# Attention of 16 heads: from half-head steps under a planner to 128 written slots

## Chip, core and metric

The kernel runs on one core of one Trainium2 chip. The metric is the device time of one execution in microseconds (us). Shapes are fixed: 1024 tokens, width 1024, 16 heads of 64, a feed-forward width of 2816, everything in float32.

## What is computed

One block of a network: a causal convolution branch and an attention branch, both fed by one normalised input, are gated and added, and a feed-forward part follows. Cut to the part that matters here:

```python
h = rms_norm(x, norm1_g)
z = h @ w_in                                  # glu_in | q | k | v | gate_logits
a = a_val * sigmoid(a_gate)
a = silu(rms_norm(causal_depthwise_conv(a, conv_w, conv_b), conv_norm_g))
y_a = a @ w_conv_out
q = rms_norm(q) * HEAD_DIM ** -0.5;  k = rms_norm(k)      # per head
# three dilated windows, mixed by their log-sum-exp: in effect one softmax
# over causal scores plus a mask per head (slope * distance + log of how many windows hold the pair)
o = softmax(q @ k.T + mask[head]) @ v
y_b = o @ w_attn_out
x = x + (sigmoid(g_a) * y_a + sigmoid(g_b) * y_b) @ w_out
x = x + ffn(rms_norm(x, norm2_g))             # up, short convolution, silu, down
```

## The kernel before

Every matmul operand is split into a high and a low part that TensorE takes in its one-pass float32 format: `split` (L74 to L77) makes the high part by a copy on ScalarE (L76) and the low part by a subtraction on VectorE (L77). A product of two such operands is three matmuls; `gemm_half` (L103 to L111) runs eight steps of three matmuls of 512 columns each into one PSUM bank, and yields after each step, so that its caller can put other work between two steps.

The stages, in order: the input norm with the gated products for the convolution (to some 200 us), the q, k and v products with their norms (to 471 us; the 31-tap convolution runs on VectorE meanwhile), the norm of the convolution's result (to 541 us), attention (to 946 us), the merge, the output product and the feed-forward part.

**Filler.** 384 steps of `gemm_half` depend little on attention: 256 steps of the gate logits (16 tiles of 128 channels by two halves of the tokens, eight steps each; `gate_steps`, L147) and 128 steps of the convolution's output product (`side_work`, L460). They are spread as filler: 24 steps right after the q, k and v products, 16 after the sum of the convolution's squares, 52 after its norm has been spread (`COVER`), then some 240 within attention by rates per half head (`FILL`), and the last 50 or so behind it. A tile's weights are loaded by SyncE (`stage`, L79), split whole (128 by 1024, L76 and L77), and its result leaves its bank by one ScalarE instruction (L152 for gates, L484 for the convolution's product) and a store.

**Attention.** `step` works on one half head (four blocks of 128 queries). It issues `score` for the four blocks of the current half, and between them the transposes (`flip`) and value products (`weigh`) of the previous half. `score(h, i)` (L502) runs two matmuls per 512 keys into a double bank of which there are two (`psA`); VectorE adds the mask and takes the row's least value in one instruction (L513), ScalarE takes the power and the row's sum (L515), VectorE inverts the sum (L516), and GpSimd scales the row block (L517). `flip` transposes one block of 128 keys for up to four query blocks into a bank (L524), copies it out high and low (L76 and L77, tiles `ph` and `pl`), and `weigh` runs two matmuls of it against the values (L532, L533), two blocks later (`PEND`), into a bank `o` that is held for the half head. The result leaves `o` by L575 and L576. All single banks, `o`, the transposes' and the filler's, come from one pool of four (`psB`).

**Order.** A planner that simulates the program sets the order of the instructions on every engine in this stretch, from the order of the program and its own durations; only two other parts of the kernel, at the very start and before the feed-forward part, are in a written order (`manual_schedule`). Each engine then runs its queue in order. Operands of a head (`head`, L487: six loads for q and k, the mask, the values; all with two buffers) are asked for by SyncE half a head before their use, and the first head's after the convolution's norm, because their memory is what the earlier stage gives up.

Of the kernel before, what the change touches and what calls it, by code (L numbers as in the profile page):

```python
# [12 lines left out]
F32 = mybir.dt.float32  # L13
# [20 lines left out]
PEND = 2  # L34
FILL = (5.5, 9.5)
COVER = (24, 16, 52)
# [14 lines left out]
def block_kernel(ctx: ExitStack, tc: tile.TileContext, x, g1, g2, pack, mask,  # L51
# [38 lines left out]
    def wpiece(src, name):  # L90
        raw = stage(src, name)
# [55 lines left out]
    def gate_steps(hT):  # L147
        def gate(c, w, half):
            gp = bank_ps(f"gate_{c}_{half}")
            yield from gemm_half(gp, w, hT, half)  # L150
            sg = cst.tile([P, 512], F32, tag="f2", bufs=2, name=f"gs_{c}_{half}")
            act.activation(sg, gp, AF.Identity, bias=pk[:, C_GB + c : C_GB + c + 1])  # L152
            sp.dma_start(dgate[c][:, half * 512 : half * 512 + 512], sg)

        for c in range(12):
            w = wpiece(w_ch[16 + c], f"gt{c}")
            for half in range(2):
                yield from gate(c, w, half)
        ws = [wpiece(w_ch[16 + c], f"gt{c}") for c in range(12, 16)]
        for half in range(2):  # L160
            for c in range(12, 16):
                yield from gate(c, ws[c - 12], half)
            if half == 0:
                yield "half"
# [19 lines left out]

    with tc.tile_pool(name="ph1", bufs=1) as p1:
        t4 = lambda name, dt=F32: p1.tile([P, 1024], dt, tag="t4", bufs=4, name=name)
# [192 lines left out]
        def qkv_head(ch, tt, ps):  # L379
# [7 lines left out]
            sq = p1.tile([P, 512], F32, tag="sq", bufs=2, name=f"sq_{ch}_{tt}")  # L387
# [5 lines left out]
            qn = p1.tile([P, 512], F32, tag="qn", bufs=3, name=f"qn_{ch}_{tt}")  # L393
# [4 lines left out]
        def qkv_tail(ch, tt, qn):  # L398
# [4 lines left out]
            qh = p1.tile([P, 512], F32R, tag="qh", bufs=2, name=f"qh_{ch}_{tt}")  # L403
            ql = p1.tile([P, 512], F32R, tag="ql", bufs=2, name=f"ql_{ch}_{tt}")
# [23 lines left out]
        gates = gate_steps(hT)  # L428
        for _ in range(COVER[0]):
            next(gates)  # L430
# [9 lines left out]
        for _ in range(COVER[1]):  # L440
            next(gates)
        for tt in range(8):
            if tt % 4 == 0:
                psr = bank_ps(f"psr_{tt}")
            dg = p1.tile([P, P], F32, tag="dg", bufs=2, name=f"dg_{tt}")
            dve.tensor_scalar(dg, ident, rs8[:, tt : tt + 1], None, op0=ALU.mult)
            pe.matmul(psr[:, (tt % 4) * P : (tt % 4 + 1) * P], ones, dg, start=True, stop=True)
            if tt % 4 == 3:
                dve.tensor_copy(sqacc[:, (tt // 4) * 512 : (tt // 4) * 512 + 512], psr)
# [5 lines left out]
        for _ in range(COVER[2]):  # L455
            next(gates)


    with tc.tile_pool(name="ph2", bufs=1, reuse_waits="tile") as p2:
        def side_work():  # L460

            left = []
            for t in gates:
                if t == "half":
                    aT = hb_tiles(hb1, "aT")
                    left = list(range(0, KT, 2))
                    wait = 0
                elif left:
                    if wait == 0:
                        load_split(aT, da, 0, "a", [left.pop(0)])  # L470
                    wait = (wait + 1) % 7
                yield
            assert not left
            left = list(range(0, KT, 2))
            for c0 in (0, 4):
                ws = [wpiece(w_co[c], f"co{c}") for c in range(c0, c0 + 4)]
                for half in range(2):
                    for c in range(c0, c0 + 4):
                        if left:
                            load_split(aT, da, 1, "a", [left.pop(0)])  # L480
                        yp = bank_ps(f"ya_{c}_{half}")
                        yield from gemm_half(yp, ws[c - c0], aT, half)
                        ya = cst.tile([P, 512], F32, tag="f2", bufs=2, name=f"ya_{c}_{half}")
                        act.activation(ya, yp, AF.Copy)  # L484
                        sp.dma_start(dya[c][:, half * 512 : half * 512 + 512], ya)

        def head(h):  # L487
            hp, r, g8 = h // 2, (h % 2) * DH, h // 8
            q = p2.tile([P, T], F32R, tag="q", bufs=2, name=f"q_{h}")
            kh = p2.tile([P, T], F32R, tag="kh", bufs=2, name=f"kh_{h}")  # L490
            kl = p2.tile([P, T], F32R, tag="kl", bufs=2, name=f"kl_{h}")
            m = p2.tile([P, T], F32, tag="m", bufs=2, name=f"m_{h}")
            v = p2.tile([P, 8, P], F32R, tag="v", bufs=2, name=f"v_{h}")
            for s in range(2):
                fetch(q[s * DH : (s + 1) * DH, :], dq[g8][s][r : r + DH, hp % 4, :])
                fetch(kh[s * DH : (s + 1) * DH, :], dk[g8][0][r : r + DH, hp % 4, :])
                fetch(kl[s * DH : (s + 1) * DH, :], dk[g8][1][r : r + DH, hp % 4, :])
            sp.dma_start(m, mask[h])
            fetch(v, dv[h // 8][:, h % 8, :, :])
            return q, kh, kl, v, m  # L500

        def score(h, tiles, i):  # L502
            q, kh, kl, v, m = tiles
            nk = (i + 1) * P
            s = big_ps(f"s_{h}_{i}")
            for c0 in range(0, nk, 512):
# [7 lines left out]
                                     op0=ALU.add, op1=ALU.min, accum_out=st[:, 0:1])  # L514
            act.activation(pt, pt, AF.Exp, bias=st[:, 0:1], scale=-1.0, accum_out=st[:, 1:2])  # L515
            dve.reciprocal(st[:, 2:3], st[:, 1:2])  # L516
            pool.tensor_scalar(pt, pt, st[:, 2:3], 1.0, op0=ALU.mult, op1=ALU.mult)  # L517
            return pt
# [12 lines left out]
        def weigh(o, v, nkt, kt, ph, pl, c):  # L531
            pe.matmul(o[:, c], v[:, kt, :], ph[:, c], start=(kt == 0), stop=False)  # L532
            pe.matmul(o[:, c], v[:, kt, :], pl[:, c], start=False, stop=(kt == nkt - 1))  # L533

        filler = side_work()
# [3 lines left out]
        def fill(n):  # L539
            credit[0] += n  # L540
            while credit[0] >= 1.0:
                credit[0] -= 1.0
                next(filler, None)

        opairs = {}

        def step(cur, prev):

            pts = []
            rate = FILL[0] / 14 if prev is not None and prev[1] else FILL[1] / 10  # L550
            if prev is not None:
                h, half, ppts, v = prev
                nkt = half * 4 + 4
                o = bank_ps(f"o_{h}_{half}")
                pend = []
            for n in range(4):
                if cur is not None:
                    pts.append(score(cur[0], cur[2], cur[1] * 4 + n))
                fill(rate)
                if prev is not None:  # L560
                    for kt in range(n * nkt // 4, (n + 1) * nkt // 4):
                        pend.append(flip(h, half, ppts, kt))
                        fill(rate)
                        if len(pend) > PEND:
                            weigh(o, v, nkt, *pend.pop(0))
            if prev is not None:
                while pend:
                    fill(rate)
                    weigh(o, v, nkt, *pend.pop(0))
                r = (h % 2) * DH  # L570
                if h % 2 == 0 and half == 0:
                    opairs[h // 2] = p2.tile([P, T], F32, tag="op", bufs=2, name=f"op_{h}")
                opair = opairs[h // 2]
                tmp = p2.tile([P, 512], F32, tag="ot", bufs=2, name=f"ot_{h}_{half}")
                act.activation(tmp[r : r + DH, :], o[DH:P, :], AF.Copy)  # L575
                dve.tensor_tensor(out=opair[r : r + DH, half * 512 : half * 512 + 512], in0=o[0:DH, :],  # L576
                                  in1=tmp[r : r + DH, :], op=ALU.add)
                if h % 2 == 1:
                    sp.dma_start(do_[:, h // 2, half * 512 : half * 512 + 512],
                                 opair[:, half * 512 : half * 512 + 512])  # L580
            return pts

        prev = None
        nxt = head(0)
        for h in range(H):
            cur = nxt
            for half in range(2):
                if half == 1 and h + 1 < H:
                    nxt = head(h + 1)
                pts = step((h, half, cur), prev)  # L590
                prev = (h, half, pts, cur[3])
        step(None, prev)
        for _ in filler:
            pass
# [5 lines left out]
    if True:  # L600
        oT = hb_tiles(hb2, "oT")
        for half in range(2):
            load_split(oT, do_, half, "o")
# [38 lines left out]
        for c0 in (0, 4):  # L642
            ws = [wpiece(w_ao[c], f"ao{c}") for c in range(c0, c0 + 4)]
# [535 lines left out]
```

## Time and profile before

| | us |
|---|---|
| median of three runs (lowest, highest) | 1790.07 (1787.41, 1792.12) |
| profiled execution | 1790.98 |
| its span, first to last instruction | 1789.2 |
| TensorE busy in the span | 1761.9 |
| VectorE, ScalarE, GpSimd busy | 1314.4, 770.9, 183.8 |

The profile is one execution. A row names the source line, the engine, the operation and the tiles, output first. A matmul's end is modelled: rows of back-to-back matmuls overlap, so the distance from one start to the next is what a matmul costs, and an engine's busy time is the union of its rows. "PEclk" is the share of full clock that TensorE was granted. An idle time in square brackets stands before the instruction that ended it, with what released it. The rows themselves stand in the prediction.

### The profile page before, as it was taken

The page shows a single profiled execution, that of the slowest core. Times are in us where ns is not written, and L with a number is a line of the kernel's source. Part 1 is how long each engine was busy: PE and PEld are TensorE (multiplying, and loading weights), DVE is VectorE, ACT ScalarE, POOL GpSimd, SP SyncE. Part 2 cuts the span into 40 slices and gives each one's busy share as a digit, 9 for nine tenths or more (in the row PEclk, how much of TensorE's full clock was granted, in tenths as well). Part 3 has the DMA queues.
Part 4 walks back from the last instruction along what each step waited for, and adds up shares of the span by engine and source line. Part 5 has one row for each costly group of instructions (what it writes and reads, how often), then busy time and mean ns, then how long its engine had stood idle before and what let it go on. Part 6 is the DMA issues. An engine that isn't in the chain of part 4 may idle for free. (4 is left out here: it accounts for less than half of the span.)

```text
span 1789.2 us, 22563 instructions
## 1 busy us (share of the span) xinstructions
PE 1761.9 (98%) x8248; PEld 1459.5 (82%) x8248; DVE 1314.4 (73%) x1805; ACT 770.9 (43%) x1203; POOL 183.8 (10%) x193
## 2 busy tenths in 40 slices
PE   8999999999999999999999999999999999999999
PEld 6888888888887888887888888888888888878887
DVE  6999999999735656665654564587777677789863
ACT  6111132232246656665655333454454454543431
POOL 1000132133002222221210000000000000000000
PEclk9999999999999999999999999999999999999999
DMA  5111145345459446664627558542222222499851
GB/s 207 47 50 56 36 142 165 112 136 162 151 193 253 138 147 177 188 186 144 177 71 264 171 197 315 193 137 83 95 83 82 83 82 83 130 322 326 293 175 47
DMA packets 146529, 272.78 MB, mean 152 GB/s; under 512 B 11761, under 2 KB 61041, under 8 KB 146418
## 3 DMA queue, kind: packets, MB, share of 16 engines
q1 hardware_dynamic: 146416, 271.34, 46.9%
q8 instruction: 65, 1.06, 0.3%
q14 instruction: 46, 0.38, 0.1%
q10 hardware_dynamic: 2, 0.00, 0.0%
HBM read 197.90 MB, written 73.40 MB: 152 GB/s over the span
## 5 line engine op out<-in xcount | busy, mean ns | idle before, releaser
L367 DVE SCALAR_TENSOR_TENSOR cacc<-apad,pk,cacc 128x1024 f32<-128x1024 f32 x240 | 298.1, 1277 | 0.7
L125 PE MATMUL qkv<-hi_qkv,hT 128*128 128x512 f32 x384 | 151.9, 397 | 0.0
L127 PE MATMUL qkv<-hi_qkv,hT 128*128 128x512 f32 x384 | 150.5, 392 | 0.0
L126 PE MATMUL qkv<-lo_qkv,hT 128*128 128x512 f32 x384 | 149.5, 390 | 0.0
L513 DVE CUSTOM_DVE_ANT_0 p<-s,m 128x128 f32<-128x128 f32 (+7 forms) x128 | 95.1, 750 | 62.8 <-PE pp L524 42.9
L77 DVE TENSOR_TENSOR pl<-pp,ph 128x512 fp32r<-128x512 f32 x192 | 102.9, 550 | 48.7 <-ACT ph L76 48.0
L76 ACT ACTIVATE ph<-pp 128x512 fp32r<-128x512 f32 x192 | 91.0, 487 | 96.1 <-PE pp L524 93.5
L517 POOL TENSOR_SCALAR p<-p,st 128x128 f32<-128x128 f32 (+7 forms) x128 | 95.3, 752 | 335.6 <-DVE st L516 277.8
L922 DVE SCALAR_TENSOR_TENSOR u<-u,pk 128x1023 f32<-128x1023 f32 x88 | 112.3, 1278 | 2.1 <-ACT u L920 1.8
L101 POOL TENSOR_TENSOR rs<-ss,mhalf 128x8 f32<-128x8 f32 x32 | 73.8, 2311 | 338.0 <-DVE ss L100 338.0
L515 ACT ACTIVATE p<-p,st 128x128 f32<-128x128 f32 (+7 forms) x128 | 99.0, 776 | 14.9 <-DVE st L513 13.1
L108 PE MATMUL gate<-hT,hi_gt 128*128 128x512 f32 x256 | 101.7, 397 | 0.0
L109 PE MATMUL gate<-hT,hi_gt 128*128 128x512 f32 x256 | 100.8, 394 | 0.0
L110 PE MATMUL gate<-hT,lo_gt 128*128 128x512 f32 x256 | 100.3, 393 | 0.0
L524 PE MATMUL pp<-ident,p 128*128 128x128 f32 x576 | 94.0, 276 | 0.0
L127 PEld LDWEIGHTS qkv<-hi_qkv,hT 128*128 128x128 f32 x384 | 72.1, 188 | 15.4
L126 PEld LDWEIGHTS qkv<-lo_qkv,hT 128*128 128x128 f32 x384 | 72.2, 188 | 14.4
L125 PEld LDWEIGHTS qkv<-hi_qkv,hT 128*128 128x128 f32 x384 | 72.1, 188 | 14.1
L77 DVE TENSOR_TENSOR lo_uv<-raw_uv,hi_uv 128x1024 fp32r<-128x1024 f32 x20 | 24.5, 1226 | 79.9 <-ACT hi_uv L76 79.9
L532 PE MATMUL o<-ph,v 128*128 128x512 f32 x192 | 73.0, 380 | 5.6 <-ACT ph L76 3.4
L524 PEld LDWEIGHTS pp<-ident,p 128*128 128x128 f32 x576 | 69.1, 142 | 10.0 <-DVE pl L77 0.2
L508 PE MATMUL s<-kh,q 128*128 128x512 f32 (+1 forms) x192 | 68.6, 362 | 7.4 <-DVE st L513 7.3
(313 smaller groups left out, 4633.6 us busy)
## 6 DMA issues: line engine op xcount, KB each, us to landing
wr<-w_down SPq DMA_DIRECT2D x45, 512.0 KB, 5.9
gr<-dff SPq DMA_DIRECT2D x62, 256.0 KB, 5.5
raw_qkv<-w_qkv SPq DMA_DIRECT2D x24, 512.0 KB, 4.1
dff<-u SPq DMA_DIRECT2D x22, 512.0 KB, 2.6
raw_uv<-w_up SPq DMA_DIRECT2D x21, 512.0 KB, 3.3
raw_ug<-w_up SPq DMA_DIRECT2D x20, 512.0 KB, 3.2
dv<-v SPq DMA_DIRECT2D x16, 512.0 KB, 3.2
raw_gt<-w_ch SPq DMA_DIRECT2D x16, 512.0 KB, 4.8
```

Of the source, the lines that this page charges most:

```text
L77: dve.tensor_tensor(out=lo, in0=src, in1=hi.bitcast(F32), op=ALU.subtract)
L108: pe.matmul(o, hi[:, k, :], ah[:, k, :], start=(k == 0), stop=False)
L109: pe.matmul(o, hi[:, k, :], al[:, k, :], start=False, stop=False)
L110: pe.matmul(o, lo[:, k, :], ah[:, k, :], start=False, stop=(k == KT - 1))
L125: pe.matmul(ps, ah, hi[:, k % 2, :], start=(k == 0), stop=False)
L126: pe.matmul(ps, ah, lo[:, k % 2, :], start=False, stop=False)
L127: pe.matmul(ps, al, hi[:, k % 2, :], start=False, stop=(k == KT - 1))
L367: dve.scalar_tensor_tensor(out=acc, in0=a[:, j : j + T], scalar=w(j), in1=acc, op0=ALU.mult, op1=ALU.add)
L515: act.activation(pt, pt, AF.Exp, bias=st[:, 0:1], scale=-1.0, accum_out=st[:, 1:2])
L517: pool.tensor_scalar(pt, pt, st[:, 2:3], 1.0, op0=ALU.mult, op1=ALU.mult)
L524: pe.transpose(pp[:, qb * P : (qb + 1) * P], pts[qb][:, kt * P : (kt + 1) * P], ident)
L922: dve.scalar_tensor_tensor(out=acc[:, d:], in0=src[:, : T - d], scalar=w(2 - d), in1=acc[:, d:], op0=ALU.mult, op1=ALU.add)
```

## The change

Attention becomes a list of 128 slots, one for each head, half and query block, in a written order on TensorE, VectorE and ScalarE. SyncE and GpSimd stay with the planner, and so does everything outside the block. In each slot, in this order: the scores of the slot's block; the inverse and the scaling of the block before (`share`); filler; the transposes of the slot five back (`BACK`: one or two blocks of keys), with filler behind each; the value products of the transposes of the slot before; the power of the slot's own block (`powers`), which so stands behind the copies of the transposes on ScalarE; the result of a half head when it is complete; filler, and one half-split on each side of it. Six slots without scores end the list.

The filler becomes one generator, `side_steps`. It asks for weights up to two tiles ahead, puts their splits into a list as halves of 512 columns (`pieces`), and each slot takes at most one half from the list, at the earliest two slots after it was asked for (`piece_high(2)`; its low half a slot later). If a tile's pieces are not done when the tile starts, they are issued there. `COVER` becomes 24, 8 and 20 steps, `FILL` eight rates that repeat with each head (17.5 steps a head, 280 in all), the tail slots take four each, and 28 steps are left behind them.

The temporary tiles of the first stages that end with q, k and v move to a pool of their own, which is given up there; the first head's q, k and mask take that memory at once and are fetched before the first filler. A head's q, k and mask are then asked for in slot 2 of the head before, its values in slot 6 of the head before (the slots of a head count from 0 to 7). The eight diagonal tiles `dg` of the convolution's norm get eight buffers instead of two. After attention, the first two weights of the merge are loaded between the two halves of the attention result.

The core of the diff:

```diff
-PEND = 2
-FILL = (5.5, 9.5)
-COVER = (24, 16, 52)
+FILL = (1.5, 3.4, 1.8, 1.9, 1.6, 3.0, 2.1, 2.2)
+BACK = 5
+COVER = (24, 8, 20)
...
+    def piece_low():
+        while half_done:
+            hi, lo, src = half_done.pop()
+            dve.tensor_tensor(out=lo, in0=src, in1=hi.bitcast(F32), op=ALU.subtract)
+            count[1] += 1
+
+    def piece_high(age=0):
+
+        if pieces and count[2] - pieces[0][3] >= age:
+            hi, lo, src, _ = pieces.popleft()
+            act.activation(hi, src, AF.Copy)
+            half_done.append((hi, lo, src))
+
+    def one_piece():
+        piece_low()
+        piece_high()
+        piece_low()
...
+        for i, (_, n, go) in enumerate(uses):
+            while len(got) < min(len(keys), keys.index(n) + 3):
+                k = len(got)
+                if k >= 4 and last[keys[k - 4]] >= i:
+                    break
+                w = ask_weights(src[keys[k]], keys[k])
+                got[keys[k]] = w, count[0]
+            w, need = got[n]
+            if n.startswith("co"):
+                need = max(need, marks[(i - 32) // 4 % 2])
+            while count[1] < need:
+                one_piece()
+            yield from go(w)
...
-            sq = p1.tile([P, 512], F32, tag="sq", bufs=2, name=f"sq_{ch}_{tt}")
+            sq = p1a.tile([P, 512], F32, tag="sq", bufs=2, name=f"sq_{ch}_{tt}")
...
-        for _ in range(COVER[0]):
-            next(gates)
+        p1a_cm.__exit__(None, None, None)
+        p2i_cm = tc.tile_pool(name="ph2i", bufs=1, side="right", reuse_waits="tile")
+        p2i = p2i_cm.__enter__()
...
+        tiles = {0: head(0)}
+        gates = side_steps(hT, da)
+
+        def cover(n):
+            for _ in range(n):
+                next(gates)
+                one_piece()
+
+        cover(COVER[0])
...
-            dg = p1.tile([P, P], F32, tag="dg", bufs=2, name=f"dg_{tt}")
+            dg = p1.tile([P, P], F32, tag="dg", bufs=8, name=f"dg_{tt}")
...
+        slots = [(h, half, n) for h in range(H) for half in range(2) for n in range(4)]
+        pts = {}
+        late = done = None
+        values(0)
+        ENG = mybir.EngineType
+        with tc.manual_schedule(engines={ENG.Activation, ENG.DVE, ENG.PE}):
+            pend = []
+            for at in range(len(slots) + BACK + 1):
+                count[2] += 1
+                cur = slots[at] if at < len(slots) else None
+                rate = FILL[at % 8] if cur else 4
                 if cur is not None:
+                    h, half, n = cur
+                    if (half, n) == (0, 2) and h + 1 < H:
+                        tiles[h + 1] = head(h + 1)
+                    if (half, n) == (1, 2) and h + 1 < H:
+                        values(h + 1)
+                    new = score(h, tiles[h], half * 4 + n)
+                    pts[h, half, n] = new[0]
+                if late is not None:
+                    share(*late)
+                fill(rate * 0.4)
+                flips = []
+                if BACK <= at < len(slots) + BACK:
+                    h, half, n = slots[at - BACK]
+                    nkt = half * 4 + 4
+                    four = [pts[h, half, i] for i in range(4)]
                     for kt in range(n * nkt // 4, (n + 1) * nkt // 4):
+                        flips.append((h, half, vals[h], *flip(h, half, four, kt)))
+                        fill(rate * 0.2)
+                for w in pend:
+                    done = weigh(*w) or done
+                pend = flips
+                late = None
+                if cur is not None:
+                    powers(*new)
+                    late = new
+                if done is not None:
+                    result(*done)
+                    done = None
+                piece_low()
+                fill(rate * (0.6 - 0.2 * len(flips)))
+                piece_high(2)
+            for _ in gates:
+                piece_low()
+                piece_high()
...
+        load_split(oT, do_, 0, "o")
+        ao_raw = [stage(w_ao[c], f"ao{c}") for c in range(2)]
+        load_split(oT, do_, 1, "o")
```

More of the change, by code (lines that the diff above doesn't have):

```diff
@@ L145, in block_kernel @@
     dform = [[dr.tile([P, 1024], F32R, name=f"dform{f}_{i}") for i in range(7)] for f in range(3)]
[L147 to L153, printed above, removed]
+    HALVES = (slice(0, 512), slice(512, 1024))
@@ new lines, in side_steps @@
+        keys = list(dict.fromkeys(n for _, n, _ in uses))
+        src = {n: w for w, n, _ in uses}
+        last = {n: i for i, (_, n, _) in enumerate(uses)}
+        got = {}
+        for i, (_, n, go) in enumerate(uses):
[11 more added lines that the diff above has]
+            yield from go(w)
@@ L439, in block_kernel @@
         rstd_of(rs8, pss[:, 0:8], D, cs8)
-        for _ in range(COVER[1]):
-            next(gates)
+        cover(COVER[1])
         for tt in range(8):
@@ L454, in block_kernel @@
             sp.dma_start(da[:, c, :], ct)
-        for _ in range(COVER[2]):
-            next(gates)
+        cover(COVER[2])
     with tc.tile_pool(name="ph2", bufs=1, reuse_waits="tile") as p2:
[L460 to L500, printed above, removed]
+        vals = {}
@@ L583, in block_kernel @@
[L583 to L594, printed above, removed]
+                next(gates, None)
+        slots = [(h, half, n) for h in range(H) for half in range(2) for n in range(4)]
```

152 lines of the change are left out of this document (98 added, 54 removed).

## The prediction

> **What bounds the kernel now.** The page's first part comes first: which engine is full.
>
> ```profile
> PE 1761.9 (98%) x8248; PEld 1459.5 (82%) x8248; DVE 1314.4 (73%) x1805; ACT 770.9 (43%) x1203; POOL 183.8 (10%) x193
> ```
>
> TensorE is busy for 98% of the span, and the change takes no matmul away. So it can only win TensorE's idle time and its slow clock in the stretch that it rewrites. The windows of that stretch (columns: length, TensorE, weight loads, VectorE, ScalarE, GpSimd, granted clock, DMA) show how much that is.
>
> ```profile
> 471.00:541.00 70.00, 69.69 (x323) 57.86 (x322) 28.58 (x33) 24.49 (x29) 1.64 (x1) 1.00 0.58 194
> 541.00:643.00 102.00, 98.54 (x535) 82.61 (x534) 61.31 (x168) 63.83 (x141) 25.96 (x36) 1.00 0.66 187
> 643.00:653.00 10.00, 8.03 (x39) 6.84 (x38) 8.36 (x22) 8.13 (x18) 3.83 (x5) 0.83 0.69 171
> 653.00:804.00 151.00, 147.75 (x808) 124.46 (x807) 93.93 (x244) 95.82 (x205) 36.55 (x50) 1.00 0.61 175
> 804.00:817.00 13.00, 8.97 (x33) 6.51 (x32) 8.67 (x13) 7.28 (x14) 1.29 (x2) 0.74 0.78 267
> 817.00:946.00 129.00, 127.35 (x690) 106.81 (x690) 73.51 (x188) 76.38 (x164) 27.64 (x36) 1.00 0.40 116
> 946.00:971.00 25.00, 25.00 (x112) 20.70 (x111) 14.70 (x14) 16.30 (x22) 0.00 (x0) 1.00 1.00 362
> ```
>
> Attention (541 to 946) lasts 405 us with 390.64 us of TensorE: 14.4 us idle. The clock fell twice: 8.03 us of work at 0.83 lost 1.4 us, 8.97 us at 0.74 lost 2.3 us, together 3.7. VectorE and ScalarE sum to 245.8 and 251.4 us, some 61% of 405, so neither bounds the stage; what costs is the order in which they come to things. The waits of this stretch say who was late (columns: total, times, longest).
>
> ```profile
> PE s L508 <- DVE st L513: 7.3, 10, 1.3
> PE o L532 <- ACT ph L76: 3.4, 3, 1.7
> PE o L532 <- DVE op L576: 1.5, 5, 0.6
> PE o L533 <- DVE pl L77: 1.2, 1, 1.2
> DVE p L513 <- DMA m<-mask: 10.3, 1, 10.3
> ```
>
> Nineteen waits make 13.4 of the 14.4 us. Half are scores that wait for a score bank, because VectorE came late to L513. The timeline at the worst place shows why.
>
> ```profile
> 805.51 1.06 ACT L76 ACTIVATE aT<-raw_a 128x1024 fp32r<-128x1024 f32 x1 [0.46 <-DMA raw_a<-da]
> 806.47 0.26 ACT L76 ACTIVATE ph<-pp 128x128 fp32r<-128x128 f32 x1
> 806.78 0.33 PE L532 MATMUL o<-ph,v 128*128 128x128 f32 x1 [1.67 <-ACT ph L76]
> 810.44 1.06 ACT L76 ACTIVATE aT<-raw_a 128x1024 fp32r<-128x1024 f32 x1 [1.44 <-DMA raw_a<-da]
> ```
>
> The planner had put whole-tile splits of the filler's operands in ScalarE's queue, their loads came late, and the copies `ph` that TensorE needed stood behind them.
>
> **The prize.** A matmul's cost is the distance between starts.
>
> ```profile
> 1633.31 5.44 PE dx L1016 x24
> 564.36 0.63 PE L524 MATMUL pp<-ident,p 128*128 128x128 f32 x4
> 564.75 0.47 PE L532 MATMUL o<-ph,v 128*128 128x512 f32 x1
> 565.06 0.39 PE L533 MATMUL o<-pl,v 128*128 128x512 f32 x1
> 500.89 0.71 PE L447 MATMUL psr<-dg,ones 128*128 128x128 f32 x4 [0.16 <-DVE dg L446]
> ```
>
> Back to back, 512 columns take 5.44 / 24 = 0.227 us, but a row is 0.39 us long, so each wait is shown 0.16 us too short: 19 times 0.16 is 3.0 us more. The prize is 14.4 + 3.7 + 3.0 = 21.1 us, and 0.3 us idle in 471 to 541, where the psr matmuls wait for a `dg` (two such gaps of 0.16; the change gives each its own buffer): 21.4 us. A filler step is three matmuls, 0.68 us. From 564.36 to 565.06 lie four transposes and one matmul: 0.70 - 0.23 = 0.47 us, 0.12 a transpose.
>
> **The change part by part.** *Filler moved.* 384 steps stay 384: 52 before attention instead of 92, 280 in the slots, 24 in the tail, 28 behind. A moved step costs the same 0.68 us wherever it runs: nothing, while its cover holds. Three covers shrink.
>
> ```profile
> 489.28 0.17 DVE L100 TENSOR_SCALAR css<-pss 128x8 f32<-128x8 f32 x1 [4.52 <-PE pss L436]
> 491.20 0.48 DVE L446 TENSOR_SCALAR dg<-ident,crs 128x128 f32<-128x128 f32 x2 [1.75 <-POOL crs L101]
> 513.05 9.17 DVE L452 TENSOR_TENSOR cacc<-cacc,sqacc 128x1024 f32<-128x1024 f32 x8
> 522.74 3.23 ACT L453 ACTIVATE cacc<-cacc,pk 128x1024 f32<-128x1024 f32 x3
> 524.95 1.58 SPq L454 DMA_DIRECT2D da<-cacc  x2
> da<-cacc SPq DMA_DIRECT2D x8, 512.0 KB, 3.3
> ```
>
> Before the psr matmuls, 8 steps (5.4 us) replace 16. The sums are there at 489.3, the wait for `crs` ends at 491.2, eight `dg` take 8 times 0.24 more, to 493.1: 3.8 us are needed, covered with 1.6 to spare. Before attention, 20 steps (13.6 us) replace 52. The last store is issued by 526.5 and lands 3.3 us later, 529.8, which is 16.8 us after VectorE began at 513.0. The first row blocks overwrite the convolution's memory, so L513 waits for these stores. TensorE needs L513's first end only at the third score, after two slots (0.12 + 0.23 us of scores and 4.9 steps, 3.7 us): 13.6 + 3.7 = 17.3 us. It fits by half a microsecond; I charge **1 us**, bounds 0 and 3 (if the last of the eight is the one overwritten, and a table load or a piece comes between). Behind the last value product, 19 us of filler stand instead of 28 and full DMA (1.00 at 946 to 971), but the merge needs only half of the attention result at first, which is complete four slots earlier: nothing; uncovered, a late load would cost some 4 us, the landing time above and a little.
>
> *First head's operands.* The mask wait of 10.3 us made TensorE idle at 541 to 546; that part is in the 14.4 already. The seven loads go to SyncE's queue ahead of the filler's, at some 472, with 38 us until their use. Nothing.
>
> *Splits in halves.* 64 halves of 512 columns take the place of 32 wholes; each instruction more adds a fixed part, but ScalarE and VectorE have 39% left. Nothing on TensorE. Eight stores move to ScalarE's queue: also in that slack.
>
> *Transposes five slots back.* The longest chain is the eighth block of a head to the first transposes that use it, two slots later.
>
> ```profile
> L513 DVE CUSTOM_DVE_ANT_0 p<-s,m 128x1024 f32<-128x1024 f32 x16 | 19.4, 1214 | 0.0
> L515 ACT ACTIVATE p<-p,st 128x1024 f32<-128x1024 f32 x16 | 18.5, 1154 | 1.8 <-DVE st L513 1.8
> L515 ACT ACTIVATE p<-p,st 128x512 f32<-128x512 f32 x16 | 11.6, 722 | 2.2 <-DVE st L513 2.1
> L515 ACT ACTIVATION_READ_ACCUMULATOR p<-p,st 128x1 f32 x128 | 24.4, 191 | 0.0
> L516 DVE RECIPROCAL st<-st 128x1 f32<-128x1 f32 x128 | 19.8, 157 | 15.6 <-ACT p L515 14.8
> L517 POOL TENSOR_SCALAR p<-p,st 128x1024 f32<-128x1024 f32 x16 | 18.0, 1128 | 10.6 <-DVE st L516 10.5
> L76 ACT ACTIVATE ph<-pp 128x512 fp32r<-128x512 f32 x96 | 56.0, 595 | 53.6 <-PE pp L524 51.6 <-PE o L533 0.6
> L152 ACT ACTIVATE gs<-gate,pk 128x512 f32<-128x512 f32 x21 | 14.3, 681 | 6.7 <-PE gate L110 6.7
> ```
>
> Scores 4 x 0.227 = 0.91, then 1.21 + 1.15 + 0.19 + 0.16 + 1.13: 4.75 us, and five hand-overs. TensorE meanwhile runs slot 7 (0.91 of scores, two transposes 0.24, two products of 384 columns 0.35, by their columns, 2.2 steps 1.50: 3.0), slot 0 (0.12 + 0.12 + 0.23 + 1.02 = 1.5), and of slot 1 0.23 of scores, one step 0.68 and three transposes of the other blocks 0.36: 5.8 us. One microsecond is left for hand-overs: **no charge**, upper bound 0.5 us in each of 16 heads, 8 us, if a half-split stands ahead of the power. All other blocks are shorter.
>
> *Banks.* The pool still has four: `o`, the filler's and two for transposes. At a tile's end the old bank waits for L152 while the new tile takes another. In a slot with two blocks of transposes (slots 1 to 4) L152 stands behind two copies and a power: 2 x 0.60 + 0.72 + 0.19 + 0.68 = 2.8 us. TensorE has about 2.6 us of work before it needs that bank (four products 0.91, 1.1 steps 0.75, scores 0.45, 0.7 steps 0.5). 0.2 us are missing; the nearest row, products that waited for a bank to be emptied (1.5 us, 5 times), says 0.3. 280 + 24 steps are 38 tile ends, and 8.7 of the 17.5 steps fall in these slots: 19 x 0.3 = **5.7 us**, bounds 0 and 19 x 0.9 = 17 (a half-split of 0.6 ahead of L152 each time).
>
> **The sum.** 1790.98 - 21.4 + 1 + 5.7 = 1776.3 for an execution like the profiled one, which is 0.9 above the median: 1775.4. I take 1775.
>
> **The clock** enters here: it fell where TensorE was idle 2 of 10 us and 4 of 13, in waits of at most 1.7 us. [...]
>
> **Rivals.** *Late loads.* ScalarE now takes pieces in written order, and nothing passes one whose load is late.
>
> ```profile
> m<-mask SPq DMA_DIRECT2D x15, 512.0 KB, 7.9
> DMA to landing us min/median/max: 4.2/7.0/9.9
> ```
>
> The second row is `raw_a`. Two slots are some 6 us (405 / 128 = 3.2 each). A load asked for beside a head's seven (two or three slots in eight) lands at up to 9.9 us: a wait of up to 4 us on ScalarE, of which TensorE's lead of about a slot hides most. 24 loads x 3/8 = 9, at 1.4 us each (the longest such wait above) 13 us: 1788. For it: 805.51; against it: a piece waits its turn in the list anyway. [...]
>
> *Banks at every tile end; slower.* If a half-split (0.6 us) stands ahead of L152 at each of the 38 ends, and one-block slots hide no more than the others, each costs 0.3 + 0.6 = 0.9: 34 us instead of 5.7, 1803, with the clock falling on top. It decides from (21.4 - 1) / 38 = 0.54 us an end. For it: the pool is full at each end by count. Against it: in before the waits on a bank's emptying came five times, none over 0.6.
>
> *No gain from the order.* The waits return as short ones, the chain above at its 8 us and banks at 11: 1788.
>
> **How the numbers follow.** Forecast, 1768 to 1783 (all charges 0, or both banks and the chain at half their bounds): 0.62. Late loads 0.10 and no gain 0.10, both near 1788. Banks, slower, 0.13. Better than the prize as I can count it, under 1768: 0.05. From 1766 to 1790 leaves out the slower rival and little else. What a measurement of this kernel can tell from no change is about 0.3%, 5.4 us: faster is under 1784.7. The forecast, the better case and a little of the two at 1788: 0.71; within: 0.15; slower: 0.14.
>
> **What would show it.** Right: 541 to 946's counterpart with TensorE idle under 7 us, a granted clock of 1.00, no row of a score waiting for L513, no wait for the first mask. Wrong: products or transposes waiting for L152 or for `pl` (banks), `hi` or `aT` copies waiting for DMA with TensorE idle behind (late loads), transposes waiting for L517 in the first half-head's slot (chain), a score waiting for `da` at the start (cover). If another stage moved by more than 2 us, the whole argument, that only this stretch changes, would be wrong.

## The result and the profile after

| | before | after |
|---|---|---|
| median (lowest to highest), us | 1790.01 (1787.41 to 1792.12) | 1774.43 (1773.15 to 1774.65) |
| profiled execution, span, us | 1790.98, 1789.2 | 1773.15, 1771.4 |
| mean granted clock | 0.997 | 1.000 |

The changed kernel takes 0.9912 of the time before (95% interval 0.9895 to 0.9929), 15.6 us less; 1775 was forecast. Three views of its profile answer to those of before. First the page's line of the engines, then the windows (length, TensorE, weight loads, VectorE, ScalarE, GpSimd, granted clock, DMA).

```profile
PE 1752.5 (99%) x8248; PEld 1451.3 (82%) x8248; DVE 1332.5 (75%) x1837; ACT 775.8 (44%) x1235; POOL 187.3 (11%) x193
```

```profile
471.00:541.00 70.00, 68.96 (x345) 57.55 (x344) 40.85 (x82) 36.64 (x64) 9.08 (x12) 1.00 0.82 255
541.00:946.00 405.00, 400.08 (x2155) 335.54 (x2154) 261.34 (x623) 255.82 (x547) 90.96 (x117) 1.00 0.58 167
946.00:971.00 25.00, 25.00 (x112) 20.71 (x111) 11.93 (x14) 8.58 (x12) 0.00 (x0) 1.00 0.71 232
```

TensorE, 14.4 us idle in 541 to 946 before, is idle there for 4.9 us now, and the granted clock is 1.00 there (0.99 before). The windows hold the same times and not quite the same work, since attention, but for one early score, now begins at 510.2 us and not at 541.0. Over the whole stretch, 471 to 971 us before and 470 to 953 us now, TensorE is idle for 14.7 and 6.0 us. From the first filler to the merge's first matmul the trace goes from 470.27 to 952.54, where it went from 471.08 to 971.02: 482.3 us for 499.9, so 17.7 of the spans' 17.8 us lie in this stretch. The waits of this stretch on TensorE (us in total, times, longest), as far as the view lists them, are these:

```profile
PE pp L598 <- ACT gs L205: 1.2, 2, 0.6
PE ya L109 <- DVE pl L78: 1.1, 1, 1.1
PE pp L598 <- DVE pl L78: 1.0, 1, 1.0
PE pp L598 <- ACT ya L216: 0.9, 2, 0.5
PE gate L109 <- DVE pl L78: 0.5, 2, 0.3
PE s L578 <- DVE st L583: 0.4, 1, 0.4
PE o L612 <- DVE pl L78: 0.3, 1, 0.3
```

Line numbers have moved: L578 and L579 are the scores, L583 VectorE's mask and least value (L513 before), L588 the power (L515), L591 and L592 inverse and scaling, L598 the transposes (L524), L612 and L613 the products, L77 and L78 the copies, L205 and L216 the instructions that empty the filler's bank, L169 and L162 the half-splits. No row of a score waiting for a score bank is left but one of 0.4 us, at 513.1 in the start, and none waits for `ph`. Nine of the ten waits are for one of the four banks, in the sense of the prediction: the bank in question is full until L205, L216 or L78 has read it. One of them in the timeline of after, with the end of the filler's tile in its first row:

```profile
530.52 0.39 PE L111 MATMUL gate<-hT,lo_gt 128*128 128x512 f32 x1
530.75 0.60 PE L598 MATMUL pp<-ident,p 128*128 128x128 f32 x4
...
531.45 0.60 ACT L77 ACTIVATE ph<-pp 128x512 fp32r<-128x512 f32 x1 [1.12 <-PE pp L598]
...
531.94 0.68 ACT L205 ACTIVATE gs<-gate,pk 128x512 f32<-128x512 f32 x1
```

The 72nd step of filler, the last of the ninth tile, has its last matmul at 530.52. Its bank could be emptied from about 530.9, but L205 starts at 531.94, behind the copy of transposes that came later; TensorE's next transposes need that bank and start at 532.68. The reason is in the code: the emptying stands behind the eighth `yield`, so it is issued only when the next step is drawn.

### The profile page after: what moved, and what is told of

The parts are those of the page before. It is cut to its first block, busy times and chain, and to the rows that moved or that the text cites. A ratio compares the mean times of both kernels' runs of the same rounds, so it can differ in the third digit from the quotient of the medians.

```text
span 1771.4 us, 22647 instructions
## 1 busy us (share of the span) xinstructions
PE 1752.5 (99%) x8248; PEld 1451.3 (82%) x8248; DVE 1332.5 (75%) x1837; ACT 775.8 (44%) x1235; POOL 187.3 (11%) x193
## 5 line engine op out<-in xcount | busy, mean ns | idle before, releaser
L77 ACT ACTIVATE ph<-pp 128x512 fp32r<-128x512 f32 x192 | 91.0, 489 | 139.4 <-PE pp L598 139.1
L78 DVE TENSOR_TENSOR pl<-pp,ph 128x512 fp32r<-128x512 f32 x192 | 103.7, 553 | 57.7 <-ACT ph L77 56.6
L583 DVE CUSTOM_DVE_ANT_0 p<-s,m 128x128 f32<-128x128 f32 (+7 forms) x128 | 96.4, 754 | 66.0 <-PE s L579 40.0
L592 POOL TENSOR_SCALAR p<-p,st 128x128 f32<-128x128 f32 (+7 forms) x128 | 98.4, 769 | 321.7 <-DVE st L591 237.7
L109 PE MATMUL gate<-hT,hi_gt 128*128 128x512 f32 x256 | 107.1, 418 | 0.6 <-DVE pl L78 0.5
L588 ACT ACTIVATE p<-p,st 128x128 f32<-128x128 f32 (+7 forms) x128 | 99.0, 774 | 8.6 <-DVE st L583 7.7
L110 PE MATMUL gate<-hT,hi_gt 128*128 128x512 f32 x256 | 100.5, 393 | 0.0
L598 PE MATMUL pp<-ident,p 128*128 128x128 f32 x576 | 90.4, 273 | 3.4 <-ACT gs L205 1.2
L598 PEld LDWEIGHTS pp<-ident,p 128*128 128x128 f32 x576 | 71.0, 140 | 24.1 <-ACT gs L205 2.5
L78 DVE TENSOR_TENSOR lo_uv<-raw_uv,hi_uv 128x1024 fp32r<-128x1024 f32 x20 | 24.5, 1225 | 79.8 <-ACT hi_uv L77 79.8
L612 PE MATMUL o<-ph,v 128*128 128x512 f32 x192 | 70.6, 371 | 0.3 <-DVE pl L78 0.3
L842 PE MATMUL xz<-blk_t,hi_s3g 128*128 128x512 f32 x176 | 68.7, 390 | 1.0 <-ACT xc L987 0.7
```

The lines of the kernel that those rows point to most:

```text
L78: dve.tensor_tensor(out=lo, in0=src, in1=hi.bitcast(F32), op=ALU.subtract)
L109: pe.matmul(o, hi[:, k, :], ah[:, k, :], start=(k == 0), stop=False)
L110: pe.matmul(o, hi[:, k, :], al[:, k, :], start=False, stop=False)
L598: pe.transpose(pp[:, qb * P : (qb + 1) * P], pts[qb][:, kt * P : (kt + 1) * P], ident)
```

## The experiments

Each kernel is compared with before on the same chip; the medians of before on these chips were 1788.98, 1789.11 and 1789.28 us. The differences from after therefore bear an uncertainty of about 1 us. The theory: the written order as a whole removes TensorE's waits, each of its three rules (lag of five, power behind the copies, spread halves) is needed, and what is left is the emptying of banks. The rivals: the gain comes from the moved filler, from the early fetch or from the smaller splits, with a planner as good as the list. Three small parts of the change were not tried alone: the merge's two weights loaded early, the eight stores in ScalarE's queue, and the eight `dg` without the early fetch.

### The list without its order

```diff
-        with tc.manual_schedule(engines={ENG.Activation, ENG.DVE, ENG.PE}):
+        if True:
```

> The changed kernel with the 128 slots as they are, but the order of ScalarE, VectorE and TensorE left to the planner again. Theory (the order as written is what keeps score banks and copies on time): the long waits come back, TensorE idles some 8 to 14 us in the rewritten stretch and the clock falls at least once, 1782 to 1790 us. Rival (halves, five slots and the early fetch do it, whoever orders them): 1773 to 1777 us, clock 1.00.

Measured: 1798.84 us, 1.0059 (1.0038 to 1.008) of before. With the same slots in the program and the planner free to order them, the kernel is 24 us slower than after and slower than before, worse than the 1782 to 1790 us that the theory allowed: TensorE is idle for 18.3 us in the window below, at a granted clock of 0.98. Its waits on TensorE (the two largest of the view), its attention window, and the worst place of its timeline:

```profile
PE s L578 <- DVE st L583: 6.2, 11, 1.3
PE pp L598 <- DVE pl L78: 3.7, 3, 2.9
```

```profile
541.00:946.00 405.00, 386.71 (x2038) 321.52 (x2037) 236.90 (x609) 239.37 (x529) 87.85 (x116) 0.98 0.52 154
```

```profile
816.35 3.10 DVE L162 TENSOR_TENSOR aT<-raw_a,aT 128x512 fp32r<-128x512 f32 x5
...
819.36 0.69 DVE L78 TENSOR_TENSOR pl<-pp,ph 128x512 fp32r<-128x512 f32 x1
...
820.11 0.47 PE L598 MATMUL pp<-ident,p 128*128 128x128 f32 x1 [2.89 <-DVE pl L78]
```

The planner put five half-splits in a row into VectorE's queue (3.10 us), and the copy `pl`, ready since `ph` was out at 816.6, stood behind them. That is the pattern of before at 805 to 811, with halves in the place of wholes. Without the written order the slots lose.

### One slot less of lag

```diff
-BACK = 5
+BACK = 4
```

> The changed kernel with transposes four slots behind instead of five. Theory (the chain from the eighth block's scores to its scaled powers is 4.75 us and some 0.5 of hand-overs; four slots back TensorE has 2.8 us of slot 7 and 0.8 of slot 0 to run meanwhile): transposes wait 1.6 us for GpSimd's scaling once in a head, 16 x 1.6 = 26 us, 1800 us (1790 to 1805). Rival (the distance has plenty of room): 1773 to 1777 us.

Measured: 1828.84 us, 1.022 (1.02 to 1.024), far above the expected range. The wait named is there, and in both halves of a head instead of one:

```profile
PE pp L598 <- POOL p L592: 40.1, 39, 1.6
```

```profile
544.84 0.82 DVE L583 CUSTOM_DVE_ANT_0 p<-s,m 128x640 f32<-128x640 f32 x1 [1.60 <-PE pp L598]
...
545.59 0.16 DVE L591 RECIPROCAL st<-st 128x1 f32<-128x1 f32 x1
...
545.91 0.69 POOL L592 TENSOR_SCALAR p<-p,st 128x512 f32<-128x512 f32 x1 [2.72 <-DVE st L591]
546.66 0.14 PEld L598 LDWEIGHTS pp<-ident,p 128*128 128x128 f32 x1 [1.86 <-POOL p L592]
```

This is a block of 512 columns, the last of a first half. Its inverse L591 stands behind L583 of the next block, as `share` is written behind the next `score`, so the chain is longer by one L583 than the prediction's sum of 4.75 us, and the shorter slots of the first half do not cover it either. At five slots that extra is covered in after, which has no row of transposes waiting for L592.

### No spreading of the splits

```diff
-                piece_low()
                 fill(rate * (0.6 - 0.2 * len(flips)))
-                piece_high(2)
```

> The changed kernel with no half-split in the slots: a filler tile's splits are all issued where the tile starts. Theory (spreading the halves is a large part of the gain): at some 20 tile starts TensorE waits 1 to 2 us for the first halves, and the ten halves ahead of the first convolution tile cost some 5 us, with copies of the transposes late behind them: 1795 to 1815 us. Rival (only the order of attention's own instructions counts): under 1780 us.

Measured: 1823.31 us, 1.0197 (1.0175 to 1.022), again above the range. A tile's pieces are issued only when the tile starts, and TensorE's filler stands for them (waits of this kernel):

```profile
PE ya L109 <- ACT hi_co L169: 15.5, 7, 4.5
PE gate L109 <- ACT hi_gt L169: 14.8, 10, 2.5
```

With waits up to 4.5 us the granted clock was 0.97 in 541 to 946 and 0.86 in 946 to 971, and 0.99 over the whole profiled execution (1.00 in after). That execution is 56 us longer than that of after; the listed waits on TensorE come to 37 us instead of 5.4, and the 0.01 of clock lost over its span of 1827 us is worth some 18 us by estimate: together 50 of the 56.

### The power ahead of the copies

```diff
                 if late is not None:
                     share(*late)
+                if cur is not None:
+                    powers(*new)
                 fill(rate * 0.4)
...
                 if cur is not None:
-                    powers(*new)
                     late = new
```

> The changed kernel with each slot's power (L588) ahead of the slot's copies of transposes on ScalarE instead of behind them. Theory (copies are what empties banks and feeds products; ahead of them stands now an instruction that waits 1.2 us for VectorE's L583 and lasts up to 1.15): each copy comes later and bank waits rise from the 5 us of the changed kernel to 8 to 15: 1777 to 1785 us. Rival (ScalarE has 37% left, its order within a slot is hidden): 1773 to 1776 us.

Measured: 1823.41 us, 1.0194 (1.0179 to 1.0209). The direction was foreseen, the size was far too small. Two waits and one place:

```profile
PE o L612 <- ACT ph L77: 10.4, 11, 1.7
PE pp L598 <- ACT gs L205: 7.1, 7, 2.0
```

```profile
739.22 0.83 ACT L588 ACTIVATE p<-p,st 128x640 f32<-128x640 f32 x1 [1.66 <-DVE st L583]
...
740.05 0.67 ACT L205 ACTIVATE gs<-gate,pk 128x512 f32<-128x512 f32 x1
740.62 0.79 ACT L77 ACTIVATE ph<-pp 128x256 fp32r<-128x256 f32 x2
...
740.77 0.33 PE L598 MATMUL pp<-ident,p 128*128 128x128 f32 x1 [1.96 <-ACT gs L205]
```

ScalarE was idle for 1.66 us at the power, because that waits for VectorE's L583, and L583 waits for TensorE's score. An instruction that depends on what TensorE has just done was put ahead of instructions that TensorE needs next. The cost is thus not only the power's own 1 us ahead of the copies, but the wait in front of it, at every slot where the score is late; the queue passes it to the emptying of banks, to the copies and back to TensorE.

### The first head's operands fetched late

```diff
-        tiles = {0: head(0)}
...
-            sp.dma_start(da[:, c, :], ct)
+            stored = sp.dma_start(da[:, c, :], ct)
+        with tc.issue_after(stored.ins):
+            tiles = {0: head(0)}
```

> The changed kernel with the first head's seven loads issued behind the last store of the convolution's norm, as late as the kernel before had them. Theory: that store is issued at 509 us in the changed kernel, loads then land at 515 and the mask at some 520, TensorE reaches the first scores at 509: 6 to 8 us lost, 1780 to 1783 us. Rival (the early fetch is worth no more than the two gaps of 2.4 us that the kernel before showed at 541 to 546): 1775 to 1778 us.

Measured: 1785.41 us, 0.9983 (0.9974 to 0.9993): 11 us more than after, a little above the theory's range, from one place. SyncE's last store of the convolution and its next load, then TensorE's first score, then the window of the start:

```profile
508.33 0.54 SPq L560 DMA_DIRECT2D da<-cacc  x1
508.96 0.72 SPq L134 DMA_DIRECT2D q<-dq  x1
...
518.84 0.44 PE L579 MATMUL s<-kh,q 128*128 128x128 f32 x1 [9.63 <-DMA kh<-dk]
```

```profile
471.00:541.00 70.00, 59.59 (x281) 49.64 (x280) 32.65 (x62) 29.02 (x45) 6.54 (x9) 0.93 0.68 219
```

TensorE waits 9.63 us for `kh`, and works at a lowered clock behind it (0.93 on average in this window). With 20 steps of cover the operands must be early.

The same delay with the old spread of the filler, 52 steps of cover:

```diff
-FILL = (1.5, 3.4, 1.8, 1.9, 1.6, 3.0, 2.1, 2.2)
+FILL = tuple(x * 15 / 17.5 for x in (1.5, 3.4, 1.8, 1.9, 1.6, 3.0, 2.1, 2.2))
-COVER = (24, 8, 20)
+COVER = (24, 16, 52)
```

First this spread alone, with the early fetch left as in after:

> The changed kernel with the filler spread as the kernel before had it: 24, 16 and 52 steps ahead of attention and 15 a head (the eight rates scaled by 15 / 17.5). Theory (a step costs 0.68 us wherever it runs, while its cover holds; slots of 22.7 us a head against 18.4 on VectorE and ScalarE still have slack): 1773 to 1777 us. Rival (the slots need the longer filler, their slack is small): above 1780 us.

Measured: 1774.45 us, 0.9914 (0.99 to 0.9927), the time of after: that filler was moved into attention wins and costs nothing that can be measured. Five slots of lag are just short here, though: with 15 steps a head one set of transposes waits 2.4 us for L592, at 796.25, and the mean granted clock of the profiled execution is 0.999 (1.000 in after). Then both:

> The changed kernel with the old spread of the filler and the first head's loads behind the convolution's last store: 52 steps, 35 us, then lie between the psr matmuls and attention. Theory (the early fetch is worth the 11 us that it was found to be only because 20 steps do not cover the loads): within 2 us of the old spread with the early fetch. Rival (it is worth some 10 us in either spread): 10 us above it.

Measured: 1779.11 us, 0.9939 (0.9926 to 0.9952), 4.7 us over the spread alone. That lies between the two expectations. Its waits on TensorE begin with

```profile
PE pp L599 <- POOL p L593: 6.0, 3, 2.8
```

One of the three, 2.4 us at 801.84, is the wait of the spread alone. The other two, 2.8 and 0.9 us, are transposes of the first head that wait for the scaling of its third and fourth blocks. The mask is not what was late: VectorE's first L584 (L583 of after) waits for the score. ScalarE was held up:

```profile
546.10 0.69 ACT L205 ACTIVATE gs<-gate,pk 128x512 f32<-128x512 f32 x1 [7.35 <-DMA dgate<-gs]
546.69 0.60 ACT L589 ACTIVATE p<-p,st 128x384 f32<-128x384 f32 x1
...
548.31 0.47 PE L599 MATMUL pp<-ident,p 128*128 128x128 f32 x1 [2.77 <-POOL p L593]
```

The emptying L205 waited 7.35 us for a free result buffer, of which there are two. The stores of the results in them stood in SyncE's queue among the heads' loads, were issued at 536.86, and landed some 9 us later; the third block's power L589 stood behind L205 on ScalarE.

The last one turns the question round: before, with nothing but the first head's q, k and mask fetched early, in a memory of their own, and eight `dg`.

```diff
-            q = p2.tile([P, T], F32R, tag="q", bufs=2, name=f"q_{h}")
...
+            q, kh, kl, m = first_keys if h == 0 else keys_of(h)
...
+        first_keys = keys_of(0)
         gates = gate_steps(hT)
...
-            dg = p1.tile([P, P], F32, tag="dg", bufs=2, name=f"dg_{tt}")
+            dg = p1.tile([P, P], F32, tag="dg", bufs=8, name=f"dg_{tt}")
```

> The kernel before with the early fetch alone: the early tiles in a pool of their own, the first head's q, k and mask asked for ahead of the filler, eight dg buffers; order, steps and spread as before. Theory (the two gaps of 2.4 us at 541 to 546 and 1 us at the psr matmuls go, the long waits of the planner's order stay): 1785 to 1788 us. Rival (the early fetch is the larger part of the gain): 1776 to 1780 us.

Measured: 1785.35 us, 0.9975 (0.9964 to 0.9987): 3.9 us of gain from this part alone, as expected. Its waits on TensorE are those of before, led by

```profile
PE s L519 <- DVE st L524: 4.7, 8, 0.8
```

(its L519 and L524 are the scores and the mask): the planner's order keeps the rest.

### Wholes for halves

```diff
-    HALVES = (slice(0, 512), slice(512, 1024))
+    HALVES = (slice(0, 1024),)
...
-            for i, c in enumerate(HALVES):
-                ask_piece(aT[0][half][:, k + i, :], aT[1][half][:, k + i, :], raw[:, c])
+            ask_piece(aT[0][half][:, k : k + 2, :], aT[1][half][:, k : k + 2, :], raw.rearrange("p (a b) -> p a b", a=2))
```

> The changed kernel with the filler's splits as wholes of 1024 columns in the list, one whole a slot at most. Theory (one instruction of 1.05 us on ScalarE or 1.22 on VectorE at a slot's end delays the next slot's by half a microsecond more than a half does, in some 40 slots, and a slot's slack takes most of it): 1775 to 1779 us. Rival (halves matter as much as the order does): above 1785 us.

Measured: 1772.7 us, 0.9909 (0.9895 to 0.9924), below the theory's range: whole pieces, one to a slot, are as good as halves, within 2 us. The halves bring nothing in this order; the place that a piece is given does.

### The banks

The emptying issued with the eighth step, not with the ninth:

```diff
+        def ahead(steps):
+            for k, _ in enumerate(steps):
+                if k < KT - 1:
+                    yield
...
-                yield from gemm_half(gp, w, hT, half)
+                yield from ahead(gemm_half(gp, w, hT, half))
...
                 sp.dma_start(dgate[c][:, half * 512 : half * 512 + 512], sg)
+                yield
```

and the same for the convolution's product.

> The changed kernel with a filler tile's emptying instruction (L205, L216) and its store issued right behind the tile's eighth step, not ahead of the next tile's first. Theory (what is left, some 5 us in eleven waits, are banks at tile ends): about half of them go, 1771 to 1773 us. Rival (the instruction waits in ScalarE's queue behind the same copies anyway): 1774 to 1775 us, no difference.

Measured: 1767.37 us, 0.988 (0.9864 to 0.9897), 7.1 us less than after and more than expected. The place of the timeline that was shown of after, in this kernel (L210 is its L205):

```profile
530.23 0.39 PE L111 MATMUL gate<-hT,lo_gt 128*128 128x512 f32 x1
...
530.66 0.69 ACT L210 ACTIVATE gs<-gate,pk 128x512 f32<-128x512 f32 x1 [0.63 <-PE gate L111]
...
531.25 0.59 ACT L77 ACTIVATE ph<-pp 128x512 fp32r<-128x512 f32 x1
```

ScalarE was idle for 0.63 us here, so the emptying costs nobody anything, and TensorE's next transposes start at 531.59 instead of 532.68.

The other way to the same end is to let tiles end only in slots with one block of transposes, at exactly two tiles (16 steps) a head:

```diff
-FILL = (1.5, 3.4, 1.8, 1.9, 1.6, 3.0, 2.1, 2.2)
-COVER = (24, 8, 20)
+FILL = (1.5, 2.875, 1.625, 1.75, 1.25, 3.0, 2.0, 2.0)
+COVER = (24, 8, 24)
...
-        credit = [0.0]
+        credit = [1e-6]
```

> The changed kernel with 16 filler steps a head instead of 17.5 (rates 1.5, 2.875, 1.625, 1.75, 1.25, 3, 2, 2; 24 steps instead of 20 ahead of attention, the other steps behind it), so that every tile ends between slots 7 and 0 or in slot 4, never beside two wide blocks of transposes. Theory (bank waits come where a tile end meets two wide blocks): the 5 us of bank waits fall under 2, 1770 to 1772 us. Rival (slots shorter by 0.13 us leave VectorE and ScalarE less slack, which costs as much): 1774 to 1778 us.

Measured: 1769.05 us, 0.989 (0.9875 to 0.9905), 5.4 us less than after; one wait of 0.2 us is left on TensorE. And the two together:

> The bank emptied right behind the eighth step together with two tiles a head. Theory (both take away the same bank waits, of which each left under 2 us): 1766 to 1768 us, little under the better one. Rival (they are different waits and add up): 1760 to 1763 us.

Measured: 1763.92 us, 0.9854 (0.9841 to 0.9868), 25.4 us under before, 10.5 under after, and the fastest kernel here. That lies between the two expectations. The edits win 7.1 and 5.4 us alone and 10.5 us together, so they take away partly the same waits. Its attention window:

```profile
541.00:946.00 405.00, 405.00 (x2189) 342.76 (x2188) 258.42 (x628) 259.75 (x555) 95.81 (x117) 1.00 0.59 175
```

TensorE is never idle in it by the rows, at full clock: in this stretch no more is to be had by order alone, as far as the profile can show.

## Why the prediction was right, point by point

*What bounds the kernel, and where the time can go.* Right. All but 0.1 us of the difference lies in the stretch named; the rest of the kernel did not move by the 2 us that were set as the limit.

*The prize, 21.4 us.* In kind right, too small in size: the kernel with both bank edits is 25.4 us under before. The correction for modelled ends was applied to the 19 waits that have a row. TensorE's rows from 471 to 971 have 32 idle gaps, 14.7 us in all, nine of them too short for the list of waits: at 0.16 us each the correction is 5.1 us and not 3.0. The clock was mis-sized too, as its paragraph below says: 4.5 us and not 3.7. That makes an estimate of 24.3 us; for the last microsecond or so, which may be waits without any idle time in the rows, no run gives the cause. After shows the same from its side: 14 gaps of 6.0 us in all make 8.2 us by this rule, and 10.5 us could still be taken out of it.

*Banks, 19 x 0.3 = 5.7 us.* The mechanism was right: nine of the ten waits left are for banks, with 5.0 us by their rows; the emptying one step earlier won 7.1 us, keeping the ends to harmless slots 5.4. The reason given, L152 (now L205) behind two copies and a power, was half of it. At the place shown one copy stood ahead of it, because the emptying was issued a step late, and this the prediction did not see in the diff. Nor did it count before's own wait for L152, one of 0.4 us.

*Two errors that cancelled.* The prize was some 4 us too small, and what is left of it after (10.5 us) was put some 4 us too low at 1 + 5.7. The forecast of 1775 came out within a microsecond for this reason too; that is luck, and the forecast deserves less trust than its distance suggests.

*The chain to the transposes, no charge.* Right, and at the edge: no wait in after, one of 2.4 us with 15 filler steps a head instead of 17.5, and 39 waits of up to 1.6 us with one slot less. The chain as counted left out L583 of the next block, which stands ahead of the inverse on VectorE.

*The start, 1 us.* Right: one score waits 0.4 us for its bank. VectorE waited 6.5 us for the store of the convolution's norm, and the two score banks and the filler cover all but that.

*The first head's operands, "nothing" beyond the 14.4.* As a term of the sum it held, but it hid a dependence: with the short cover the early fetch is worth 11 us, with the old one 4.7, and 3.9 on the kernel before. With the short cover and without the early fetch, 3.6 us of the change's gain are left; with the old cover, 10.2.

*Moved filler, nothing; halves, nothing.* Right, by 1774.45 us and 1772.7.

*The clock, 3.7 us of the prize.* Right in kind: in after it is 1.00 in all three windows. The size was low, because the wide windows spread the fall over work done at full clock. In before the falls are 648.87 to 652.28 and 809.30 to 816.13; TensorE is busy for 3.36 and 5.65 us in them, at 0.50, and half of these 9.0 us is 4.5 us.

*The rivals.* Late loads did not come: no wait of ScalarE for the filler's loads is in the trace; a piece is two slots old before it is taken. "No gain from the order" is refuted by the list without its order, which is 24 us slower. The slower rival's mechanism, something ahead of L152 on ScalarE, exists, but it takes more than a half-split: with the power ahead of the copies it costs 49 us.

## What to carry to other kernels

An order written by hand pays as a whole: the planner with the same slots was 24 us worse, and each rule of the list (how far the transposes lag, where the power stands, when splits are taken) was worth 49 to 54 us when it alone was undone. Each of these three kernels is slower than the planner's, so a written order with one rule wrong is worse here than none. Behind a shared bank's last matmul issue its emptying at once, not when a generator is next drawn; and on an engine that runs its queue in order, as ScalarE did at 739.22 (1.66 us idle at the power, with L205 and L77 behind it), never put an instruction that waits for the newest matmul ahead of one that the next matmul needs. Where matmul ends are modelled, each wait is shown too short (by 0.16 us here: rows of 0.39 us start 0.227 us apart) and the shortest are not listed: take what a kernel without them gains as the measure, not the sum of the rows.

## What the runs showed of the hardware

*The granted clock.* It was 1.00 around a single wait of 1.62 us, and 0.58 behind waits of 0.90 and 1.17 us with 0.3 us of work between them. Windows of the kernel with a lag of four (length, TensorE, weight loads, VectorE, ScalarE, GpSimd, granted clock, DMA):

```profile
544.00:547.00 3.00, 1.38 (x10) 1.06 (x9) 0.91 (x3) 0.00 (x0) 0.69 (x1) 1.00 0.00 0
840.90:843.40 2.50, 0.43 (x3) 0.18 (x2) 0.41 (x3) 1.44 (x3) 2.02 (x2) 1.00 0.92 298
843.40:846.80 3.40, 3.40 (x14) 3.02 (x15) 1.64 (x3) 2.43 (x6) 0.00 (x0) 0.58 1.06 228
```

The first window holds the wait at 546.66 shown above, with 1.62 us idle, at a clock of 1.00. A second of that length, with TensorE idle for 1.62 us in 827 to 830, has 1.00 in its window and 1.00 behind it, in 829.4 to 832.9. In the window from 840.9 on TensorE is idle for 2.07 of 2.5 us, and in the 3.4 us that follow the mean clock is 0.58. In the old spread of the filler, whose longest wait on TensorE is 2.4 us, the mean over the profiled execution was 0.999; with the late operands on top of that spread, with a longest wait of 2.8 us, it was 0.998 (1.000 in after).

In before the clock was 0.50 from 648.87 to 652.28 and from 809.30 to 816.13, for 3.41 and 6.83 us. In the 3.41 us ahead of these two places TensorE's rows show 1.92 and 2.08 us of idle time. No run varied the idle time alone, so what brought the clock down is not shown.

*VectorE beside GpSimd.* A half-split's subtraction reads two tiles, the operand and its high part. The tile's row in after from 555 us on (least, median, longest ns, first and last start) and one place in its timeline:

```profile
L162 DVE TENSOR_TENSOR lo_gt<-raw_gt,hi_gt x18: 673/834/1578, 555.0 to 731.5; 128x512 fp32r<-128x512 f32 x18
```

```profile
529.03 1.13 POOL L592 TENSOR_SCALAR p<-p,st 128x1024 f32<-128x1024 f32 x1 [0.38 <-DVE st L591]
...
529.65 1.04 DVE L162 TENSOR_TENSOR lo_gt<-raw_gt,hi_gt 128x512 fp32r<-128x512 f32 x1
```

The same subtraction takes 0.67 us at best and up to 1.58, and this one, which starts during the scaling on GpSimd, takes 1.04. Of the 64 half-splits of after, the 42 that run beside no instruction of GpSimd take 0.67 to 0.69 us; all that take longer, 18 of the other 22, overlap one. No run took the scaling away from beside it, so the cause is not shown.
